# Heads of a gated delta rule in a fixed order on three engines, with right sides summed in PSUM and an inverse completed in two halves

## The chip, the cores and the metric

The kernel runs on one core of a Trainium2 chip. The metric is the device time of the core in microseconds, the median of three runs. A profile is of one execution.

## The reference

One residual block of a hybrid network on 1024 tokens of width 1024. After a normalisation, one projection feeds two branches, a gated linear attention (GLA, 4 heads) and a gated delta rule (GDN, 8 heads of 128). They are merged through sigmoid gates, projected, and followed by a squared-ReLU MLP. The change is in the GDN heads:

```python
d_qkv = jax.nn.silu(causal_short_conv(d_qkv, gdn_conv_w))   # 4 taps
d_q, d_k = l2_norm(d_q), l2_norm(d_k)
...
a_mat = jnp.where(strict, jnp.einsum('bhnid,bhnjd->bhnij', kb, k) * decay_mat, 0.0)
rhs = jnp.concatenate([v * beta[..., None], kb * jnp.exp(gc)[..., None]], axis=-1)
sol = lax.linalg.triangular_solve(a_mat + eye, rhs, left_side=True, lower=True)
u, w = sol[..., :dv], sol[..., dv:]
att = jnp.einsum('bhnid,bhnjd->bhnij', q, k) * decay_mat

def step(state, inp):                                        # over chunks
    v_new = uu - w @ state
    o = q_dec @ state + att @ v_new
    state = dec * state + k_state.T @ v_new
    return state, o

o_d = rms_norm(o_d, gdn_onorm_w) * jax.nn.silu(d_g)
```

## The kernel before

Activations lie transposed in SBUF, channels on partitions and 1024 tokens along the free axis. Dense products are computed with operands split into a high and a low part (`hH`, `hL` for the activations, `wH`, `wL` for weights): for each of 8 slices k of the contracted axis, three pairs of 128x512 matmuls, `hH,wH`, `hL,wH` and `hH,wL`. `dense_b` (L406) does one block of 128 output channels in that way. After each k it calls `tick()`: the clock of the program moves on by one, and functions that were entered in an agenda with `at(ticks, function)` for that time are issued. So small work is placed between dense work by hand: a tick is the time of three dense pairs, and each block has eight of them.

A GDN head (`gdn_head`, L741) has three dense blocks, for q (`psq`), v (`psv`) and the gate (`psg`), 24 ticks in all. Around them, in the agenda:

- the chunk's inverse `U` of 128x128 is completed from two solved 64x64 blocks: u1 transposes on VectorE, u2 and u3 are 8 products of 64x64 each on TensorE, with `yn` on VectorE between them;
- q and v pass the convolution (a scaled copy on ScalarE, then three taps on VectorE, all into `cv`) and silu; `att` makes the attention of 8 chunks of 128 tokens, `token_sums` the sums of squares of q by way of `sqt` and `sqr`;
- `kb` (scaled keys, VectorE) and `U` give `WT` (two groups on TensorE, copied by ScalarE); v is transposed and scaled into `bv`;
- a chain over the 8 chunks, one every three ticks: c1(t) sums `U`·`bv` and `WT`·`st` in PSUM and ScalarE takes it out as `vn`; c2(t), a tick later, makes the new state `st` (VectorE) and the output `po`, which ScalarE squares and copies to `ob`;
- at the end the norm (14 small steps and a product with `ob` on VectorE), 16 transposes of 32x256 to `obT`, and a product with the gate `si` (`fin`).

The chain of head h starts when its three dense blocks are through, and so lies beside the dense blocks of head h+1. Its last c2 is in the last tick of that head, and `fin` lies in the head after. `aacc` is a sum on VectorE for the modulation, that goes on beside all this, `wL` the low part of a weight tile, for the next dense block. GLA's last transposes (from `go`) fall into head 0.

An object `InOrder` stands in front of each engine and records each operation (so all have L38 in the profile). With its flag `strict` set, each operation is told to stay behind the one that the program wrote before it on that engine. In the heads the flag is off, and a scheduler, working from its own estimates, orders each engine's instructions.

Of the kernel before, what the change touches and what calls it, by code (L numbers as in the profile page):

```python
# [8 lines left out]
F32 = mybir.dt.float32  # L9
# [41 lines left out]
def block_kernel(ctx: ExitStack, tc: tile.TileContext, x, c, ada_w, ada_b, pre_mix_w, post_mix_w,  # L51
# [332 lines left out]
    plan += [(w_in, c0 + h * 128, 128, 8, V) for h in range(8) for c0 in (C_DQ, C_DV, C_DG)]  # L384
    plan += [(w, j * 256, 256, 8, None) for w in (w_bgla, w_bgdn) for j in range(4)]

    def splits():
        for w, c0, n, kt, E in plan:
            raw = load_raw(w, c0, n)
            if kt == 4:  # L390
# [95 lines left out]
    be_d = dr.tile([8, 1024], F32, name="be_d")  # L486
    dec_d = dr.tile([64], F32, name="dec_d")
# [5 lines left out]
    beC = cp.tile([128, 64], F32, name="beC")  # L493
    decB = cp.tile([128, 64], F32, name="decB")
# [189 lines left out]
    def key_norms():  # L684
        V.tensor_scalar(ssK, ssK, EPS, None, ALU.add)
        r = rsqrt(ssK, 64)
        V.tensor_mul(rbC, r, betaC)
        V.tensor_mul(beC, beC, r)
        V.scalar_tensor_tensor(beC, beC, -1.0, rbC, ALU.mult, ALU.mult)
        V.scalar_tensor_tensor(nbrC, rbC, -1.0, r, ALU.mult, ALU.mult)  # L690
        ps = pat()
        T.transpose(ps[0:64, 0:128], nbrC, ident)
        nb = t4((128, 128), p="nbr")
        V.tensor_copy(nb[0:64], ps[0:64, 0:128])
        ST.dma_start(be_d.rearrange("h (t q) -> (h t) q", q=128), nb[0:64])
# [45 lines left out]
    def gdn_head(h):  # L741

        U = Ub[h % 2]
# [4 lines left out]
        DMA.dma_start(a21, a21_d[h])  # L748
        kT, Dt = t4(p="kT"), t4(p="Dt", tag="hd")
        DMA.dma_start(kT, kT_d[h])  # L750
        DMA.dma_start(Dt, Dt_d[h])
        z = {}

        def u1():
            t11 = z["t11"] = t4((64, 8, 64), p="t11")
            lo, hi = slice(0, 32), slice(32, 64)
            for a_ in (lo, hi):
                for b_ in (lo, hi):
                    V.transpose(t11[b_, :, a_], U[a_, :, b_])

        def u2():
            py = pat()
            for t in range(NT):
                T.matmul(py[64:128, t * 64:(t + 1) * 64], a21[:, t, :], z["t11"][:, t, :], start=True, stop=True)
            z["yn"] = t4((128, 8, 64), p="yn")
            V.tensor_tensor(z["yn"][64:128], py[64:128, :].rearrange("p (t q) -> p t q", t=8),
                            colb(nbrC[64:128, h * 8:h * 8 + 8], 8, 64), ALU.mult)

        def u3():
            pu = pat()  # L770
            for t in range(NT):
                T.matmul(pu[0:64, t * 64:(t + 1) * 64], z["yn"][64:128, t, :], U[64:128, t, 64:128], start=True, stop=True)
            A.copy(U[0:64, :, 64:128], pu[0:64, :].rearrange("p (t q) -> p t q", t=8))

        at(5, u1)
        at(9, u2)
        at(11, u3)
        psq = dense_b(h_rhs)

        q = silu_half(conv(psq, h))  # L780
        vq = small(8, "vq")
        qj = t4(p="qj")
        attT = t4(p="attT")

        def att(hf):
            pt = pat()
# [3 lines left out]
            V.tensor_mul(attT[:, hf * 512:(hf + 1) * 512], pt, Dt[:, hf * 512:(hf + 1) * 512])  # L790

        at(6, lambda: att(0))
        at(7, lambda: att(1))
        at(8, lambda: A.activation(qj, q, AF.Square))
        token_sums(qj, vq, QT, EPS)
# [3 lines left out]
        kb = t4(p="kb")  # L799
        if h == 7:  # L800
            oa_s.plan(range(9, 17), 8)
        at(5, lambda: V.tensor_tensor(r3(kb), r3(ktok), colb(beC[:, h * 8:h * 8 + 8], 8), ALU.mult))
        psv = dense_b(h_rhs)

        A.activation(eg, eg, AF.Exp)
        vv = silu_half(conv(psv, 16 + h))
        bv = t4(p="bv")
        V.tensor_tensor(eg, q, eg, ALU.mult)
        qd = eg

        WT = t4(p="WT")

        def wt_(hf):
            pt = pat()
            for i in range(4):
                t = hf * 4 + i
                T.matmul(pt[:, i * 128:(i + 1) * 128], kb[:, t * 128:(t + 1) * 128], U[:, t, :], start=True, stop=True)
            A.copy(WT[:, hf * 512:(hf + 1) * 512], pt)

        at(2, lambda: wt_(0))  # L820
        at(3, lambda: wt_(1))

        def vt_(hf):
            pt = pat()
            for i in range(4):
                t = hf * 4 + i
                T.transpose(pt[:, i * 128:(i + 1) * 128], vv[:, t * 128:(t + 1) * 128], ident)
            V.tensor_tensor(r3(bv)[:, hf * 4:hf * 4 + 4, :], r3(pt, 4),
                            colb(rbC[:, h * 8 + hf * 4:h * 8 + hf * 4 + 4], 4), ALU.mult)

        at(6, lambda: vt_(0))
        at(7, lambda: vt_(1))
        psg = dense_b(h_rhs)

        sg = silu_twice(psg)
        ob = t4(p="ob")
        so = small(8, "so")
        c = {"st": None}

        def c1(t):  # L840

            sl = slice(t * 128, (t + 1) * 128)
            pv = pat()
            T.matmul(pv[:, :128], U[:, t, :], bv[:, sl], start=True, stop=(t == 0))
            if t:
                T.matmul(pv[:, :128], WT[:, sl], c["st"], start=False, stop=True)

            v2 = c["vn"] = sm.tile([128, 256], F32, tag="gst", name=nm("vn"), bufs=3)
            if t < NT - 1:
                A.activation(v2[:, 0:128], pv[:, :128], AF.Copy, scale=ksC[:, h * 8 + t:h * 8 + t + 1])  # L850
            A.copy(v2[:, 128:256], pv[:, :128])

        def c2(t):
            sl = slice(t * 128, (t + 1) * 128)
            i, hf, st, vs, vn = t % 4, t // 4, c["st"], c["vn"][:, 0:128], c["vn"][:, 128:256]
            if t < NT - 1:
                pS = pat()
                T.matmul(pS[:, :128], ktok[:, sl], vs, start=True, stop=True)
                sn = c["st"] = sm.tile([128, 128], F32, tag="st", name=nm("st"), bufs=3)
                if t:  # L860
                    V.scalar_tensor_tensor(sn, st, decB[:, h * 8 + t:h * 8 + t + 1], pS[:, :128], ALU.mult, ALU.add)
                else:
                    A.copy(sn, pS[:, :128])
            if i == 0:
                c["po"] = pat()
            po = c["po"]
            T.matmul(po[:, i * 128:(i + 1) * 128], attT[:, sl], vn, start=True, stop=(t == 0))
            if t:
                T.matmul(po[:, i * 128:(i + 1) * 128], qd[:, sl], st, start=False, stop=True)
            if i == 3:  # L870
                for i in range(4):
                    t_ = hf * 4 + i
                    A.activation(ob[:, t_ * 128:(t_ + 1) * 128], po[:, i * 128:(i + 1) * 128], AF.Square,
                                 accum_out=so[:, t_:t_ + 1])
                A.copy(ob[:, hf * 512:(hf + 1) * 512], po)
            if t == NT - 1:

                V.tensor_scalar(so, so, 1.0 / 128, None, ALU.mult)
                V.scalar_tensor_tensor(so, vq, 128.0 * EPS, so, ALU.mult, ALU.add)
                rf = rsqrt(so, 8)  # L880
                V.tensor_tensor(r3(ob), r3(ob), colb(rf, 8), ALU.mult)

        obT = t4(p="obT")

        def fin(q):
            blocks(r3(obT), r3(ob), (32 * q,))
            if q == 3:
                V.scalar_tensor_tensor(sg, obT, don, sg, ALU.mult, ALU.mult)
# [978 lines left out]
```

## Time and profile before

| | us |
|---|---|
| median of 3 runs | 1967.45 |
| lowest, highest | 1963.69, 1969.73 |
| the profiled execution | 1963.2 |
| its span | 1961.5 |
| TensorE's busy time | 1921.7 |
| mean granted clock of TensorE | 0.994 |

The heads of the GDN run from about 665 to 1062 us of the span. In rows of the timeline the first number is the start, the second the time from the first instruction's start to the last one's end, then the engine, the operation, what it writes and reads, and a count; matmuls overlap, so their pace is read from starts.

### The profile page before, as it was taken

The page shows a single profiled execution, that of the slowest core. Times are in us where ns is not written, and L with a number is a line of the kernel's source. Part 1 is how long each engine was busy: PE and PEld are TensorE (multiplying, and loading weights), DVE is VectorE, ACT ScalarE, POOL GpSimd, SP SyncE. Part 2 cuts the span into 40 slices and gives each one's busy share as a digit, 9 for nine tenths or more (in the row PEclk, how much of TensorE's full clock was granted, in tenths as well). Part 3 has the DMA queues.
Part 4 walks back from the last instruction along what each step waited for, and adds up shares of the span by engine and source line. Part 5 has one row for each costly group of instructions (what it writes and reads, how often), then busy time and mean ns, then how long its engine had stood idle before and what let it go on. Part 6 is the DMA issues. An engine that isn't in the chain of part 4 may idle for free.

```text
span 1961.5 us, 26008 instructions
## 1 busy us (share of the span) xinstructions
PE 1921.7 (98%) x9894; PEld 1622.6 (83%) x9894; DVE 1447.3 (74%) x2653; ACT 801.9 (41%) x1427; POOL 172.1 (9%) x120
## 2 busy tenths in 40 slices
PE   5999999999999999999999999999999999999998
PEld 4788888889899888888888888888888888888886
DVE  7867599658769697888787434666668886787887
ACT  5554323342342333333336231247644446343333
POOL 3300100310110100000001110000012220000001
PEclk8999999999999999999999999999999999999999
DMA  9365622423222433333358785244666767452525
GB/s 295 111 211 178 202 101 84 143 65 108 60 70 76 143 111 105 116 117 114 96 162 208 184 192 124 102 131 159 205 216 214 245 228 258 158 204 66 202 97 97
DMA packets 214444, 292.24 MB, mean 149 GB/s; under 512 B 33695, under 2 KB 153966, under 8 KB 214318
## 3 DMA queue, kind: packets, MB, share of 16 engines
q1 hardware_dynamic: 174910, 243.50, 38.1%
q10 hardware_dynamic: 21760, 35.01, 5.0%
q0 software_dynamic: 17648, 12.06, 4.7%
q8 instruction: 78, 1.28, 0.3%
q14 instruction: 48, 0.39, 0.1%
HBM read 215.42 MB, written 75.11 MB: 148 GB/s over the span
## 4 chain that ended last, share of the span: by engine, by line
PE 46%; DVE 3%; DMA 1%; ACT 0%; issue 0%; DVEq 0%; ACTq 0%
PE pa L38 23%; PE pm L38 23%; DVE obT L38 1%; DVE cv L38 0%; DMA sl<-sg_d 0%; DMA os<-oa_d 0%; DVE oL L38 0%; DVE rt L38 0%; DVE si L38 0%; DVE sqt L38 0%; DVE ya L38 0%; DVE rs L38 0%; DVE sqr L38 0%; DVE yg L38 0%; DVE st L38 0%
## 5 line engine op out<-in xcount | busy, mean ns | idle before, releaser
L38 PE MATMUL pm<-hH,wH 128*128 128x512 f32 x1008 | 327.6, 405 | 0.4 <-DVE cv L38 0.4
L38 PE MATMUL pm<-hL,wH 128*128 128x512 f32 x1008 | 314.5, 393 | 0.0
L38 PE MATMUL pm<-hH,wL 128*128 128x512 f32 x1008 | 313.5, 391 | 0.1
L38 PEld LDWEIGHTS pm<-hH,wL 128*128 128x128 f32 x1008 | 189.4, 188 | 41.8 <-DVE wL L38 0.5
L38 PEld LDWEIGHTS pm<-hL,wH 128*128 128x128 f32 x1008 | 189.6, 188 | 40.9
L38 PE MATMUL pa<-w,yH 128*128 128x512 f32 x688 | 212.1, 390 | 0.0
L38 ACT CAST wH<-raw 128x1024 fp32r<-128x1024 f32 x95 | 99.1, 1051 | 270.7 <-PE pm L38 189.1
L38 PEld LDWEIGHTS pm<-hH,wH 128*128 128x128 f32 x1008 | 176.7, 190 | 26.4 <-issue 1.1
L38 DVE TENSOR_TENSOR w<-raw,w 128x512 fp32r<-128x512 f32 (+1 forms) x142 | 123.4, 872 | 49.3 <-ACT w L38 48.5
L38 PEld LDWEIGHTS pa<-w,yH 128*128 128x128 f32 x688 | 129.1, 188 | 27.2 <-DVE ya L38 0.4
L38 ACT CAST w<-raw 128x512 fp32r<-128x512 f32 (+1 forms) x143 | 98.2, 708 | 88.9 <-DVE raw L38 79.8
L38 PE MATMUL pa<-w,yL 128*128 128x512 f32 x344 | 133.9, 389 | 0.0
L38 PE MATMUL pa<-oB,w 128*128 128x512 f32 x480 | 111.4, 390 | 0.0
L38 DVE SCALAR_TENSOR_TENSOR cv<-pm,ccol,cv 128x1023 f32<-128x1023 f32 (+2 forms) x72 | 92.1, 1280 | 24.2 <-ACT cv L38 23.1
L38 DVE TENSOR_TENSOR wL<-raw,wH 128x1024 fp32r<-128x1024 f32 x72 | 88.5, 1236 | 26.9 <-ACT wH L38 26.6
L38 PEld LDWEIGHTS pa<-oB,w 128*128 128x128 f32 x480 | 89.8, 188 | 18.5 <-DVE w L38 0.2
L38 PE MATMUL pa<-oT,w 128*128 128x512 f32 x384 | 90.8, 389 | 0.0
L38 PE MATMUL pm<-oT,w 128*128 128x512 f32 x384 | 90.8, 389 | 0.0
L38 DVE TENSOR_TENSOR ya<-pa,ya 128x512 f32<-128x512 f32 x82 | 55.9, 689 | 43.3 <-PE pa L38 43.3
L38 PEld LDWEIGHTS pa<-oT,w 128*128 128x128 f32 x384 | 72.1, 188 | 14.9
L38 PEld LDWEIGHTS pm<-oT,w 128*128 128x128 f32 x384 | 72.1, 188 | 14.9
L38 PE MATMUL pm<-oH,wH 128*128 128x512 f32 x256 | 80.7, 396 | 0.0
(329 smaller groups left out, 3808.7 us busy)
## 6 DMA issues: line engine op xcount, KB each, us to landing
yL<-y_d SPq DMA_DIRECT2D x53, 512.0 KB
raw<-in_mlp_w_dram SPq DMA_DIRECT2D x23, 1024.0 KB
raw<-in_w_in_dram SPq DMA_DIRECT2D x19, 1024.0 KB
raw<-in_w_in_dram SPq DMA_DIRECT2D x34, 512.0 KB
araw<-in_ada_w_dram SPq DMA_DIRECT2D x32, 512.0 KB
raw<-in_mlp_w_dram SPq DMA_DIRECT2D x18, 512.0 KB
araw<-in_ada_w_dram SPq DMA_DIRECT2D x32, 256.0 KB
sg_d<-sig ACTq DMA_DIRECT2D x16, 512.0 KB
```

The costliest lines, as they stand in the source:

```text
L38: r = fn(*args, **kw)
```

## The change

**Order.** During the eight heads `strict` is on for TensorE, VectorE and ScalarE: these three carry out the program's order. Inside a head, ticks are now counted from its begin (`on`). The convolution's taps, tanh and silu have a tick each, the norm is at tick 48, its product at 49 and the transposes at 50 and 51 (before, in effect at 52, 53, 60 and 62). High and low parts of the heads' weights are made at given ticks (`conv_w_later`).

**Right sides.** `kb`, `bv` and `WT` are gone. `ke` holds the transposed keys with a negative factor for each token. c0(t) transposes a chunk of v into PSUM and adds `ke`·`st`; ScalarE takes the sum out with the factor beta as `rs`; c1(t), a tick later, is `U`·`rs`; c2(t) stays in the tick that it had.

**Inverse.** u2 and u3 alternate between the upper and the lower 64 rows and columns of the array, chunk by chunk, with a second copy of a block of `U` (`u22`) loaded for it. They come at ticks 7 and 9, before at 9 and 11.

The first place is on VectorE, where head h's finish (`ob`, `obT`) meets the chain of head h+1 (`st`). `sqt`, `sqr` and `vq` are the sums of squares of head h+1, `t` and `uw` the inverse's transposes of head h+2, `am` small steps of the modulation. Before:

```order
L38 TENSOR_TENSOR ob_7476<-ob_7476,rs_7869 128x1024
L38 TENSOR_REDUCE sqr_7938<-sqt_7937 128x16
L38 STREAM_TRANSPOSE obT_7478<-ob_7476 32x8x32 x8
L38 TENSOR_TENSOR am_123<-pa_7981,vcol 128x8
L38 SCALAR_TENSOR_TENSOR st_7994<-st_7943,decB,pa_7992 128x128
L38 SCALAR_TENSOR_TENSOR am_123<-am_123,vcol 128x8
L38 STREAM_TRANSPOSE t_7998<-U_5855 32x8x32 x4
L38 STREAM_TRANSPOSE obT_7478<-ob_7476 32x8x32 x8
L38 TENSOR_TENSOR wL_8210<-raw_8207,wH_8209 128x1024
L38 TENSOR_SCALAR vq_7611<-pa_8027 32x8 x4
L38 SCALAR_TENSOR_TENSOR st_8035<-st_7994,decB,pa_8033 128x128
L38 SCALAR_TENSOR_TENSOR si_7472<-obT_7478,vcol,si_7472 128x1024
```

and now:

```order
L38 SCALAR_TENSOR_TENSOR rs_7001<-rt_7002,rs_7001 128x8
L38 SCALAR_TENSOR_TENSOR si_7019<-si_7019,pm_6903 128x512 x2
L38 TENSOR_TENSOR ob_6815<-ob_6815,rs_7001 128x1024
L38 STREAM_TRANSPOSE obT_7055<-ob_6815 32x8x32 x16
L38 SCALAR_TENSOR_TENSOR si_6599<-obT_7055,vcol,si_6599 128x1024
L38 STREAM_TRANSPOSE sqt_7095<-qj_6884 128x512
L38 TENSOR_REDUCE sqr_7096<-sqt_7095 128x16
L38 SCALAR_TENSOR_TENSOR st_7110<-st_7065,decB,pa_7084 128x128
L38 STREAM_TRANSPOSE uw_7027<-U_5860 32x8x32 x4
```

The new state of c2(1) stood between two halves of the sixteen transposes, and the product with the gate stood behind the next state; now all of the finish is ahead of that state.

The second place is on TensorE at the same boundary, in the first c2 and c0 of head h+1 that use a state made by VectorE: `pm` rows are dense pairs, three to a tick.

```order
L38 MATMUL pa_7504<-vn_7520,kt_7175 128x128
L38 MATMUL pa_7487<-vn_7520,attT_7280 128x128
L38 MATMUL pa_7487<-st_7485,eg_7176 128x128
L38 MATMUL pm_7455<-hH_634,wH_7336 128x512 x2
L38 MATMUL pm_7455<-hL_635,wH_7336 128x512 x2
L38 MATMUL pm_7455<-hH_634,wL_7396 128x512 x2
L38 MATMUL pa_7547<-ident,cv_7318 128x128
L38 MATMUL pa_7547<-st_7530,ke_7179 128x128
L38 MATMUL pm_7455<-hH_678,wH_7336 128x512 x2
```

c2(1) is followed by one tick of dense work, and then c0(2) reads the state that VectorE makes from c2(1). In the program before, two ticks lay between:

```order
L38 MATMUL pa_7555<-vn_7542,kt_7188 128x128
L38 MATMUL pa_7519<-vn_7542,attT_7187 128x128
L38 MATMUL pa_7519<-st_7517,eg_7189 128x128
L38 MATMUL pm_7493<-hH_632,wH_7345 128x512 x2
L38 MATMUL pm_7493<-hL_633,wH_7345 128x512 x2
L38 MATMUL pm_7493<-hH_632,wL_7346 128x512 x2
L38 MATMUL pm_7493<-hH_676,wH_7345 128x512 x2
L38 MATMUL pm_7493<-hL_677,wH_7345 128x512 x2
L38 MATMUL pm_7493<-hH_676,wL_7346 128x512 x2
L38 MATMUL pa_7578<-bv_7340,U_5855 128x128
L38 MATMUL pa_7578<-st_7557,WT_7342 128x128
```

Each group of the chain moved from two groups and a free tick to three groups, one a tick. From the head's last c2 to that c0(2) the program has seven ticks of dense pairs, the groups c0(0), c1(0), c2(0), c0(1), c1(1) and c2(1), and the transpose of c0(2).

The third place is VectorE in head 0, from the first tap of q to the attention. Before:

```order
L38 SCALAR_TENSOR_TENSOR cv_5945<-pm_5871,ccol,cv_5945 128x1023
L38 SCALAR_TENSOR_TENSOR cv_5945<-pm_5871,ccol,cv_5945 128x1022
L38 SCALAR_TENSOR_TENSOR cv_5945<-pm_5871,ccol,cv_5945 128x1021
L38 TENSOR_TENSOR yn_5983<-pa_5974,nbrC 64x512
L38 STREAM_TRANSPOSE obT_5997<-go_5596 32x4x32 x3
L38 SCALAR_TENSOR_TENSOR cv_5945<-si_5950,cv_5945 128x1024
L38 STREAM_TRANSPOSE obT_5997<-go_5596 32x4x32 x13
L38 TENSOR_TENSOR kb_5960<-kt_5956,beC 128x1024
```

and now:

```order
L38 SCALAR_TENSOR_TENSOR cv_5961<-pm_5874,ccol,cv_5961 128x1023
L38 SCALAR_TENSOR_TENSOR cv_5961<-pm_5874,ccol,cv_5961 128x1022
L38 STREAM_TRANSPOSE obT_6008<-go_5601 32x4x32 x8
L38 SCALAR_TENSOR_TENSOR cv_5961<-pm_5874,ccol,cv_5961 128x1021
L38 TENSOR_TENSOR wL_6026<-raw_5970,wH_6000 128x1024
L38 STREAM_TRANSPOSE obT_6008<-go_5601 32x4x32 x8
L38 SCALAR_TENSOR_TENSOR si_5761<-obT_6008,vcol,si_5761 128x512
L38 SCALAR_TENSOR_TENSOR aacc_4592<-araw_5925,sc,aacc_4592 128x1024
L38 SCALAR_TENSOR_TENSOR cv_5961<-si_6024,cv_5961 128x1024
L38 TENSOR_TENSOR attT_6051<-pa_6052,Dt_5869 128x512
```

Silu of q (the `cv` from `si`), which stood behind three of the sixteen transposes of GLA, is now behind all of them, the weight's low part and `aacc`.

The diff, cut to its core:

```diff
-    plan += [(w_in, c0 + h * 128, 128, 8, V) for h in range(8) for c0 in (C_DQ, C_DV, C_DG)]
+    plan += [(w_in, c0 + h * 128, 128, 8, E) for h in range(8) for c0, E in ((C_DQ, (1, 6)), (C_DV, (1, 7)), (C_DG, (2, 4)))]
...
+    def conv_w_later(raw_ap, shape, dh, dl):
+        w = [None, None]
...
+        at(dh, high)
+        at(dl, low)
+        return w
...
+        begin = clock[0]
+        def on(t, fn):
+            at(begin + t - clock[0], fn)
...
+        halves = (slice(64, 128), slice(0, 64))
         def u2():
             py = pat()
             for t in range(NT):
-                T.matmul(py[64:128, t * 64:(t + 1) * 64], a21[:, t, :], z["t11"][:, t, :], start=True, stop=True)
...
+                T.matmul(py[halves[t % 2], t // 2 * 64:t // 2 * 64 + 64], a21[:, t, :], t11[:, t, :], start=True, stop=True)
+            V.tensor_tensor(yn, r3(py[:, 0:256], 4), colb(nbrX[:, h * 4:h * 4 + 4], 4, 64), ALU.mult)
...
-        at(5, u1)
-        at(9, u2)
-        at(11, u3)
+        on(5, u1)
+        on(7, u2)
+        on(9, u3)
...
+            for s_ in (1, 2, 3):
+                on(t + s_, lambda s_=s_: tap(s_))
+            on(t + 4, tanh)
+            on(t + 5, lambda: V.scalar_tensor_tensor(y, u["t"], 1.0, y, ALU.add, ALU.mult))
...
+        ke = t4(p="ke")
+        DMA.dma_start(ke, ner_d[h].partition_broadcast(128))
...
+        on(16, lambda: V.tensor_tensor(ke, kT, ke, ALU.mult))
+        on(28, lambda: token_part(0))
+        on(30, lambda: token_part(1))
+        on(32, token_total)
...
-        at(2, lambda: wt_(0))
-        at(3, lambda: wt_(1))
...
+        def c0(t):
+            sl = slice(t * 128, (t + 1) * 128)
+            pv = c["pv"] = pat()
+            T.matmul(pv[:, 0:128], vv[:, sl], ident, start=True, stop=(t == 0), is_transpose=True)
+            if t:
+                T.matmul(pv[:, 0:128], ke[:, sl], c["st"], start=False, stop=True)
+            rs = c["rs"] = sm.tile([128, 128], F32, tag="rs", name=nm("rs"), bufs=2)
+            A.activation(rs, pv[:, 0:128], AF.Copy, scale=rbC[:, h * 8 + t:h * 8 + t + 1])
         def c1(t):
-            T.matmul(pv[:, :128], U[:, t, :], bv[:, sl], start=True, stop=(t == 0))
-            if t:
-                T.matmul(pv[:, :128], WT[:, sl], c["st"], start=False, stop=True)
...
+            T.matmul(pv, U[:, t, :], c["rs"], start=True, stop=True)
...
         for t in range(NT):
-            at(3 * t + 1, lambda t=t: c1(t))
-            at(3 * t + 2, lambda t=t: c2(t))
-        for q in range(4):
-            at((28, 29, 36, 38)[q], lambda q=q: fin(q))
+            on(24 + 3 * t, lambda t=t: c0(t))
+            on(25 + 3 * t, lambda t=t: c1(t))
+            on(26 + 3 * t, lambda t=t: c2(t))
+        on(48, norm)
+        on(49, scale)
+        for i in range(4):
+            on((50, 50, 51, 51)[i], lambda i=i: fin(i))
...
+    for e in (T, V, A):
+        e.last, e.strict = e.recent, True
     for h in range(8):
         gdn_head(h)
+    for e in (T, V, A):
+        e.strict = False
```

More of the change, by code (lines that the diff above doesn't have):

```diff
@@ L748, in gdn_head @@
         DMA.dma_start(a21, a21_d[h])
+        uw = t4((128, 16, 64), p="uw")
+        t11, yn, u22 = uw[0:64, 0:8, :], uw[:, 8:12, :], uw[0:64, 12:16, :]
+        DMA.dma_start(u22, ud[1].rearrange("j (t e) i -> e j t i", e=2)[1])
         kT, Dt = t4(p="kT"), t4(p="Dt", tag="hd")
@@ L789, in att, with squares, token_part, token_total @@
                 T.matmul(pt[:, i * 128:(i + 1) * 128], kT[:, sl], q[:, sl], start=True, stop=True)
[L790 to L795, printed above, removed]
+            V.tensor_mul(z["att"][:, hf * 512:(hf + 1) * 512], pt, Dt[:, hf * 512:(hf + 1) * 512])
+        def squares():
+            z["qj"] = t4(p="qj")
+            A.activation(z["qj"], q, AF.Square)
+        def token_part(hf):
+            if not hf:
+                z["t"], z["r"] = t4(p="sqt"), small(32, "sqr", 2)
+            h_ = slice(hf * 512, (hf + 1) * 512)
+            V.transpose(z["t"][:, h_], z["qj"][:, h_])
+            V.reduce_sum(z["r"][:, hf * 16:(hf + 1) * 16], r3(z["t"][:, h_], 16), axis=mybir.AxisListType.X)
+        def token_total():
+            ps = pat()
+            T.matmul(ps[:, 0:32], quad.rearrange("p a b -> p (a b)"), z["r"], start=True, stop=True)
+            for i in range(4):
+                V.tensor_scalar(vq[32 * i:32 * i + 32], ps[32 * i:32 * i + 32, 0:32].rearrange("p (t c) -> p c t", c=4)[:, i],
+                                EPS, None, ALU.add)
         ktok, eg = t4(p="kt", tag="hd"), t4(p="eg")
@@ L809, in gdn_head @@
[L809 to L818, printed above, removed]
-        at(2, lambda: wt_(0))
-        at(3, lambda: wt_(1))
[L823 to L829, printed above, removed]
```

123 lines of the change are left out of this document (74 added, 49 removed).

## The prediction

> **What bounds the kernel now.** I read the page first, for the engine that has no idle time.
>
> ```profile
> PE 1921.7 (98%) x9894; PEld 1622.6 (83%) x9894; DVE 1447.3 (74%) x2653; ACT 801.9 (41%) x1427; POOL 172.1 (9%) x120
> PE   5999999999999999999999999999999999999998
> PEclk8999999999999999999999999999999999999999
> ```
>
> TensorE works 98% of the span, at nine tenths or more of its clock in all slices but the first. So the change pays in two coins only: TensorE time that it takes away or adds, and TensorE idle time. A busy share says nothing about a single wait, so next come the waits of TensorE in the stage that is changed (the heads, 664 to 1100 us), and two instants that give the length of a head: the group that writes the inverse's product from `t` and `a`, in head 1 and in head 7.
>
> ```profile
> PE pa L38 <- DVE yn L38: 4.9, 5, 1.3
> PE pa L38 <- DVE st L38: 0.7, 2, 0.5
> PE pa L38 <- ACT vn L38: 0.4, 1, 0.4
> PE pa L38 <- DVE bv L38: 0.4, 1, 0.4
> 722.65 1.14 PE L38 MATMUL pa<-t,a 64*64 64x64 f32 x16
> 1021.68 1.14 PE L38 MATMUL pa<-t,a 64*64 64x64 f32 x16
> 722.65:771.50 48.85, 48.77 (x293) 41.89 (x293) 36.54 (x65) 17.85 (x46) 0.00 (x0) 1.00 0.36 105
> ```
>
> Six heads take 1021.68 - 722.65 = 299.03 us, 49.8 each, and in all eight TensorE waits 4.9 + 0.7 + 0.4 + 0.4 = 6.4 us. The last row is one head (busy us of TensorE, its loads, VectorE, ScalarE, GpSimd, then clock): VectorE, the engine waited for, has 12 us free in a head. It is late at moments, not on the whole. Whether it is late after the change is therefore a question of order inside a head.
>
> **Taken from TensorE.** The `WT` groups go, two a head.
>
> ```profile
> 943.05 1.05 PE L38 MATMUL pa<-U,kb 128*128 128x128 f32 x8
> 943.86 0.71 PE L38 MATMUL pm<-hH,wH 128*128 128x512 f32 x2
> 944.41 0.63 PE L38 MATMUL pm<-hL,wH 128*128 128x512 f32 x2
> ```
>
> Eight records take 943.86 - 943.05 = 0.81, and the dense pair behind them 944.41 - 943.86 = 0.55, where a pair in the rows of a whole tick below takes a third of 1.38, 0.46: 0.09 more. So a group costs 0.90, a record 0.1125. The rest keeps its records: a head had 16 in `WT`, 8 transposes of `vv`, and 30 in c1, 54 in all; it will have 22 in c0 (8 transposes, 7 times 2 for `ke` by `st`) and 16 in c1, 38 in all. c2 and the attention stay. 16 records x 8 heads x 0.1125 = **-14.4**.
>
> The old waits of 6.4 go too: `bv` no longer exists, `yn` has two ticks before its reader and half the columns, and the wait for `st` is worked out anew below. **-6.4**. If `yn` were as late as before, 4.9 of this would stay.
>
> u2 and u3 of the inverse now go to alternating 64-row tiles.
>
> ```profile
> 677.54 1.14 PE L38 MATMUL pa<-t,a 64*64 64x64 f32 x16
> 678.61 0.73 PE L38 MATMUL pm<-hH,wH 128*128 128x512 f32 x2
> 539.27 0.33 PE L38 MATMUL pa<-zm,b 128*64 128x64 f32 x4
> 539.38 0.28 PE L38 MATMUL pa<-zm,ks 128*64 128x64 f32 x2
> 539.50 0.34 PE L38 MATMUL pa<-zm,b 128*64 128x64 f32 x4
> ```
>
> On one tile 16 records take 1.07, or 0.067 each. No row shows tiles that differ in rows and columns; the nearest alternates 64-column tiles, 6 records in 539.50 - 539.27 = 0.23, or 0.039 each. By that a group saves 16 x 0.028 = 0.45, and 16 groups **-7.2**. Bounds: two tiles wholly beside each other, 0.53 a group, -8.6; or a record as dear as one of 128x128, 0.1125, +11.7. I take the nearest row.
>
> **Hidden.** The row of one head shows ScalarE at 17.85 of 48.85 us: 64 more scalings to `rs` (about 0.28 each by the row below, 2.2 a head) find room, and the two copies to `U` replace one. The extra loads (`ke`, `u22`) go out on SP's queue eight and nine ticks, 11 us, ahead of use; the share of the DMA engines in that row is 0.36. Uncovered, a late `ke` would hold all of c0. The split weights now come up to two ticks before use, not eight: a late `wL` would cost up to its own 1.2. The store of `od` only moves forward, behind its producer on ScalarE's queue. The mixing of `kb` (1.2) becomes that of `ke`; two `bv` of 0.69 leave VectorE.
>
> **Added: the order on VectorE.** These are the rows at the end of a head, of TensorE, ScalarE and then VectorE.
>
> ```profile
> 1004.21 0.60 PE L38 MATMUL pa<-ident,cv 128*128 128x128 f32 x4
> 1006.04 0.62 PE L38 MATMUL pm<-hH,wH 128*128 128x512 f32 x2
> 1007.42 0.38 PE L38 MATMUL pa<-bv,U 128*128 128x128 f32 x2
> 1004.41 0.28 ACT L38 ACTIVATE ob<-pa 128x128 f32<-128x128 f32 x1 [2.01 <-PE pa L38]
> 1005.59 0.17 DVE L38 TENSOR_SCALAR so<-so 128x8 f32<-128x8 f32 x1
> 1007.61 0.17 DVE L38 TENSOR_TENSOR rt<-rs 128x8 f32<-128x8 f32 x1
> 1008.37 0.68 DVE L38 SCALAR_TENSOR_TENSOR si<-si,pm 128x512 f32<-128x512 f32 x1
> 1008.97 0.16 DVE L38 SCALAR_TENSOR_TENSOR rs<-rt,rs 128x8 f32<-128x8 f32 x1
> 1009.04 0.70 DVE L38 STREAM_TRANSPOSE sqt<-qj 128x512 f32<-128x512 f32 x1
> 1009.67 1.18 DVE L38 TENSOR_TENSOR ob<-ob,rs 128x1024 f32<-128x1024 f32 x1
> 1010.77 0.68 DVE L38 TENSOR_REDUCE sqr<-sqt 128x16 f32<-128x512 f32 x1
> 1016.13 0.35 DVE L38 SCALAR_TENSOR_TENSOR st<-st,decB,pa 128x128 f32<-128x128 f32 x1
> 1018.19 3.59 DVE L38 STREAM_TRANSPOSE obT<-ob 32x256 f32<-32x256 f32 x8
> 1021.82 1.29 DVE L38 SCALAR_TENSOR_TENSOR si<-obT,vcol,si 128x1024 f32<-128x1024 f32 x1
> 1023.02 0.68 DVE L38 TENSOR_SCALAR vq<-pa 32x8 f32<-32x8 f32 x4
> ```
>
> A tick (three dense pairs) is 1007.42 - 1006.04 = 1.38. The head's last c2 is over at 1004.21, where the transposes behind it start; the norm starts 1.38 later, when ScalarE's squares are in. Before, the scheduler put `st` of the next head's c2(1) between the two halves of the sixteen transposes (1016.13), and TensorE's waits for `st` were the 0.7 us above. In the changed program all of the old head's finish stands ahead of this `st`, as the first order excerpt shows. By starts, on VectorE: 14 small steps of the norm at (1007.61 - 1005.59)/11 = 0.18, 2.6; two `si` of 0.60, 1.2; `ob` 1.1; sixteen transposes at (1021.82 - 1018.19)/8 = 0.454, 7.25; the product with `si` 1.2; `sqt` 0.63 and `sqr` 0.60; `st` 0.35. Sum 14.9, so `st` is there 1.38 + 14.9 = 16.3 after the last c2.
>
> TensorE wants it sooner than before, since c0 comes a tick ahead of the old c1. Between the last c2 and the product of `ke` and `st` in c0(2) stand, by the second excerpt, 7 ticks (9.66) and 19 small records (2.14): 11.8. It is first in TensorE's queue, and all dense pairs behind it wait. **Stall 4.5, in the boundaries into heads 2 to 7 (6 of them): +27.0.** Boundaries with an `aacc` (row below, 1.3 each) in the pile are two: **+2.6**. Bounds: if the pile only lasted as in the quoted head (`st` done 12.3 after the last c2), 0.5 a boundary, 3; if VectorE also has a step of 1.3 running each time, 35.
>
> **Head 0** has GLA's transposes in its line; these are VectorE's, and the attention that reads the result.
>
> ```profile
> 668.37 5.04 DVE L38 STREAM_TRANSPOSE obT<-go 32x128 f32<-32x128 f32 x16
> 678.05 3.91 DVE L38 SCALAR_TENSOR_TENSOR cv<-pm,ccol,cv 128x1023 f32<-128x1023 f32 x3
> 683.68 1.23 DVE L38 SCALAR_TENSOR_TENSOR cv<-si,cv 128x1024 f32<-128x1024 f32 x1
> 690.88 1.28 DVE L38 SCALAR_TENSOR_TENSOR aacc<-araw,sc,aacc 128x1024 f32<-128x1024 f32 x1
> 686.85 1.05 PE L38 MATMUL pa<-cv,kT 128*128 128x128 f32 x8
> ```
>
> The scheduler let the three taps, then silu at 683.68, pass thirteen transposes. By the third excerpt they will not: from 678.05, taps 3.9, sixteen transposes 5.0, `wL` 1.2, `si` 0.7, `aacc` 1.25, silu 1.15 end at 691.3. TensorE is at the attention at 686.85, less the 0.45 saved in u2. **+4.9**, with 0 as the other end if the old order's margins held.
>
> **The clock.** Idle TensorE has a second price. One gap of 2.6 us shows it; the second row is the window of time behind it (busy us of the engines, then the granted clock).
>
> ```profile
> 82.39 0.66 PE L38 MATMUL pa<-ident,cv 128*128 128x128 f32 x4 [2.60 <-DVE cv L38]
> 83.48:86.90 3.42, 3.42 (x12) 2.72 (x11) 1.90 (x5) 3.17 (x15) 1.43 (x1) 0.50 0.29 119
> ```
>
> After it 3.42 us ran at clock 0.50: 1.71 of work lost. The gaps of up to 1.3 in the waits above left the clock at 9 tenths or more. A gap of 4.5 to 4.9 is nearer to the first; as a part of the slow window can fall into the gap itself I take 1.5 each, seven gaps, **+10.5** (bounds 0 and 2.4 each, 16.8).
>
> The Trainium skill ("TensorE: Matmul & The Clock Gate", Part 1, the table of clock states) has the clock fall only after at least one idle window of about 3.4 us. Taken as a wholly idle window, a gap of 4.5 holds one in a third of the phases, and the clock would cost 7 x 1.71 / 3 = 4 instead of 10.5, by an estimate from that page: a time of 1978, on the way to the rival without clock loss. The trace doesn't agree: its gap of 2.60 us was enough.
>
> **Sum.** -14.4 - 6.4 - 7.2 + 27.0 + 2.6 + 4.9 + 10.5 = **+17.0**. The profiled execution has a span of 1961.5 and a time of 1963.2, 4 below the median of 1967.45: 1980.2 on its own basis, **1984** on the median's.
>
> **Rivals.**
> - *The pile doesn't hold TensorE* (faster). The point is 11.8 - 1.38 = 10.4 us from norm to `st`. For it: before, 12.3 was nearly enough, and VectorE has 12 us free per head. Against: the rows add to 14.9, and nothing may pass. Then 1967.45 - 28.0, plus head 0's 4.9 and 1.5: **1946**. That TensorE isn't really kept in that place, because the writer's order is not the program's, is out: the excerpts are of the program.
> - *Stalls, but no clock loss*: 1984 - 10.5 = **1974**, just outside what counts as slower. For it: no gap in the heads' stage now is long enough to test it there.
> - *More of the same*: the tiles save nothing (+7.2), the clock costs 2.4 (+6.3): **1998**. A c0 comes one tick (1.38) behind the c2 that makes its `st`, so any VectorE step of 1.3 at the wrong moment adds to it, which the `aacc` row (1.3) makes likely.
> - *The change doesn't do what it says*: excluded for the order; the dropped groups are gone from it.
>
> **How the numbers follow.** Forecast 0.45, no clock loss 0.21, more 0.16, no stall 0.18. A measurement here tells a change of about 0.3%, 6 us, from none. Faster: the no-stall case, 0.18. The same: two thirds of the case without clock loss, 0.14. Slower: 0.68. The range leaves out most of the no-stall case and little above: from the 1974 case with half of its stalls (some 12 less) to just past the 1998 case, 1961 to 2002.
>
> **What would show it.** Right: in the changed profile TensorE's largest wait is for `st`, six times 4 to 6 us, once a head, with the sixteen `obT` directly ahead of it on VectorE; the wait for `cv` in head 0; a granted clock under 0.99 in the heads; heads of 51 to 53 us. Wrong: no wait for `st` over 1 us, or heads of 46 to 47. The tiles: u2 near 0.62 a group. It would all be wrong if a transpose or the norm ran much faster back to back than in these rows.

## The result and the profile after

The changed kernel takes 1998.4 us (median of 5 runs, 1993.46 to 1999.87) against 1967.45; the ratio is 1.015, with a 95% interval of 1.0131 to 1.0168. It is 31 us slower by the medians, 29.5 by the ratio, where 17 were forecast; the time is inside the range of 1961 to 2002. The page of the changed kernel's profile, the lines that answer to those of before:

```profile
span 1998.2 us, 25761 instructions
PE 1924.5 (96%) x9767; PEld 1616.0 (81%) x9767; DVE 1441.1 (72%) x2638; ACT 818.1 (41%) x1483; POOL 171.2 (9%) x120
PE   5999999999999898999989999999999999999998
PEclk8999999999999999889999999999999999999999
```

TensorE has fewer matmuls (9767, before 9894) and a little *more* busy time. That is the first sign of the clock: the same work takes longer in some stretches, and slices 17 and 18 show it. The waits of TensorE in the heads (655 to 1140 us; total, times, longest):

```profile
PE pa L38 <- DVE st L38: 29.1, 8, 5.7
PE pa L38 <- DVE cv L38: 5.4, 1, 5.4
PE pm L38 <- DVE cv L38: 2.7, 1, 2.7
PE pa L38 <- DVE uw L38: 0.3, 1, 0.3
```

The old waits for `yn`, `bv` and `vn` are gone, and 6.4 us of waiting has become 37.5. One boundary of heads in the timeline (start, us, instruction, idle time before it and who ended it), TensorE and then VectorE:

```profile
814.82 0.39 PE L38 MATMUL pa<-st,eg 128*128 128x128 f32 x2
826.77 0.27 PE L38 MATMUL pa<-ident,cv 128*128 128x128 f32 x1
831.53 0.80 PE L38 MATMUL pa<-st,ke 128*128 128x128 f32 x2 [4.49 <-DVE st L38]
816.42 0.17 DVE L38 TENSOR_SCALAR so<-so 128x8 f32<-128x8 f32 x1 [3.28 <-ACT ob L38]
821.38 7.18 DVE L38 STREAM_TRANSPOSE obT<-ob 32x256 f32<-32x256 f32 x16
828.60 1.28 DVE L38 SCALAR_TENSOR_TENSOR si<-obT,vcol,si 128x1024 f32<-128x1024 f32 x1
831.14 0.34 DVE L38 SCALAR_TENSOR_TENSOR st<-st,decB,pa 128x128 f32<-128x128 f32 x1
```

The next dense pair starts at 814.96, where the last c2 is over. TensorE has done c0(2)'s transpose at 827.04 (826.77 + 0.27), 12.1 us later, and then waits; VectorE starts the norm at 816.42 and has `st` ready at 831.48, 16.5 us after that c2. All sixteen transposes (821.38) and the product with `si` (828.60), the last step of the old head's finish, stand ahead of it. Where an `aacc` lies in the pile the wait is 5.69 and 5.58; in one boundary (941.53) it is 2.7, since sixteen small products of the modulation took 1.7 us of TensorE just before and filled that part of the wait.

What the wait does to the clock shows in windows of 3.41 us. The clock changes only at the edges of such windows: all changes of it in the heads are whole multiples of 3.413 us apart. The same boundary (length, then busy us of TensorE, its loads, VectorE, ScalarE, GpSimd; granted clock; DMA):

```profile
827.37:830.78 3.41, 0.00 (x0) 0.00 (x0) 3.31 (x6) 0.00 (x0) 0.00 (x0) 1.00 0.02 8
830.78:834.20 3.42, 2.67 (x7) 2.25 (x8) 3.31 (x8) 0.37 (x1) 0.00 (x0) 0.50 0.35 145
834.20:837.61 3.41, 3.41 (x23) 2.72 (x22) 2.82 (x4) 0.52 (x2) 0.00 (x0) 0.50 0.02 5
837.61:841.02 3.41, 3.41 (x13) 3.02 (x13) 1.78 (x7) 1.11 (x1) 0.00 (x0) 0.50 0.84 243
841.02:844.43 3.41, 3.41 (x30) 2.73 (x30) 2.05 (x2) 1.00 (x3) 0.00 (x0) 1.00 1.07 353
```

The third of these windows again, counting on TensorE only the products that read or write `uw` (u2, with 64 rows):

```profile
834.20:837.61 3.41, 1.12 (x16) 0.50 0.02 5
```

One gap is followed by three windows at half clock, 2.67 + 3.41 + 3.41 us of work of which half, 4.7 us, is lost. The wait of 4.49 costs 9.2. Added up in the same way over the heads, 21.9 us are lost to the clock; before, none were.

### The profile page after: what moved, and what is told of

Its sections match the earlier page's. It is cut to its first block, busy times and chain, and to the rows that moved or that the text cites. A ratio compares the mean times of both kernels' runs of the same rounds, so it can differ in the third digit from the quotient of the medians.

```text
span 1998.2 us, 25761 instructions
## 1 busy us (share of the span) xinstructions
PE 1924.5 (96%) x9767; PEld 1616.0 (81%) x9767; DVE 1441.1 (72%) x2638; ACT 818.1 (41%) x1483; POOL 171.2 (9%) x120
## 4 chain that ended last, share of the span: by engine, by line
PE 87%; DVE 8%; DMA 2%; ACT 1%; issue 1%; SPq 0%; DVEq 0%
PE pm L38 57%; PE pa L38 30%; DVE obT L38 3%; DVE si L38 1%; DMA araw<-in_ada_w_dram 1%; DVE cv L38 1%; DVE acc L38 1%; DMA gr<-gc_d 0%; DMA x<-in_x_dram 0%; DVE ob L38 0%; DVE lba L38 0%; DVE aacc L38 0%; DVE sqr L38 0%; DVE sqt L38 0%; SPq L227 0%
## 5 line engine op out<-in xcount | busy, mean ns | idle before, releaser
L38 PE MATMUL pm<-hH,wH 128*128 128x512 f32 x1008 | 335.2, 414 | 2.7 <-DVE cv L38 2.7
L38 ACT ACTIVATE rs<-pa,rbC 128x128 f32<-128x128 f32 x64 | 23.7, 370 | 147.7 <-PE pa L38 141.2
```

The lines of the kernel that those rows point to most:

```text
L38: r = fn(*args, **kw)
```

## The experiments

Each kernel ran beside the kernel before on the same chip, and its ratio is to that. "Waits" are TensorE's idle us between 655 and 1140 us of the profile; "clock" is the work lost there, the sum over short slices of TensorE's busy time by the part of the clock that was missing.

| kernel | median, us | ratio (95%) | waits | clock |
|---|---|---|---|---|
| before | 1967.45 | 1 | 6.4 | 0 |
| the change | 1998.4 | 1.015 (1.0131 to 1.0168) | 37.5 | 21.9 |
| 1 idle work in the waits | 1986.4 | 1.0101 (1.0074 to 1.0128) | 17.1 | 7.0 |
| 2 no flag | 1969.2 | 1.0014 (1.0002 to 1.0027) | 16.9 | 3.4 |
| 3 no flag, late finish | 1956.6 | 0.9947 (0.9927 to 0.9966) | 13.2 | 0 |
| 4 TensorE without flag | 1987.0 | 1.0102 (1.0081 to 1.0124) | 21.9 | 20.2 |
| 5 flag on TensorE alone | 2003.3 | 1.0182 (1.016 to 1.0204) | 47.3 | 13.4 |
| 6 spread | 1968.7 | 1.0013 (1.0000 to 1.0026) | 20.3 | 4.5 |
| 7 spread more | 1954.9 | 0.9938 (0.9917 to 0.9958) | 11.9 | 0 |
| 8 no pile | 1951.2 | 0.9917 (0.9898 to 0.9935) | 8.9 | 4.5 |
| 9 u2 a tick later | 1989.8 | one run | 36.3 | 15.3 |
| 10 seven, on one tile | 1960.6 | 0.9965 (0.9953 to 0.9978) | 10.6 | 0 |
| 11 seven, with GpSimd | 1957.2 | 0.9948 (0.9933 to 0.9963) | 12.9 | 0 |

Spans less waits and clock (and less the added work in 1) are 1934 to 1946 us in every kernel of the new form but the tenth, where part of the form is undone. So these two columns hold most of the differences, which are 52 us between the fastest and the slowest.

**1. Does the clock cost what the windows say?** The wait stays as long, and is filled with products that nobody reads.

```diff
             pv = c["pv"] = pat()
+            for _ in range(16 if t == 2 and 1 <= h <= 6 else 0):
+                T.matmul(pv[:, 384:512], ident, ident, start=True, stop=True)
```

> The changed kernel, with 16 idle products of the identity with itself (128x128, into unused columns of PSUM, read by nobody) put on TensorE ahead of c0(2) in heads 1 to 6, so that 3.6 us of each wait for st are filled with work. If the lost clock is a price of TensorE's idling, the half-clock stretches behind these waits (17.9 us of lost work in the profile of the changed kernel) go, the waits that are left are 0.9 to 2 us each, and the time falls by 16 to 18 us, to about 1981. If the low clock has another cause (heat, the position in the program), or costs nothing that ends up in the time, the time stays within 4 us of 1998.

The same boundary in its timeline:

```profile
824.37 3.73 PE L38 MATMUL pa<-ident 128*128 128x128 f32 x32
829.14 0.49 PE L38 MATMUL pa<-st,ke 128*128 128x128 f32 x2 [0.93 <-DVE st L38]
```

Work of 3.6 us and 0.93 of idling stand where 4.49 of idling stood, `st` is no sooner, and the clock stays at full behind it (the product itself takes 0.49, in the change 0.80). The lost clock falls from 21.9 to 7.0, the span from 1998.2 to 1983.6, the median by 12.0 (by the ratios 0.5%, 10 us), less than the 16 to 18 expected: head 0's gap (2.2 us of clock), one gap with an `aacc` (1.7) and the end of head 7 (3.0) still lowered the clock, and the added work outlasts the one short wait of 2.7. The price of the clock is shown to be one of idling; the wait itself, which this kernel keeps, is the other part.

**2. Is it the flag or the ticks?**

```diff
-    for e in (T, V, A):
-        e.last, e.strict = e.recent, True
...
-    for e in (T, V, A):
-        e.strict = False
```

> The changed kernel without the flag that keeps the three engines to the program's order; all ticks as in the change. If the order given by the ticks makes the stall, the sixteen transposes still stand ahead of st and the time is 1998 within 6 us, with waits for st of 4.5 us. If the flag makes it (the scheduler would otherwise let st pass), the waits for st shrink to under 1 us and the time is about 1950.

Neither expectation was right. The time is that of the kernel before, as if the ticks were harmless, but the waits don't vanish. TensorE and VectorE at the same boundary:

```profile
801.60 0.39 PE L38 MATMUL pa<-st,eg 128*128 128x128 f32 x2
813.61 0.27 PE L38 MATMUL pa<-ident,cv 128*128 128x128 f32 x1
815.21 0.68 PE L38 MATMUL pa<-uw,a 64*64 64x64 f32 x16
820.65 0.49 PE L38 MATMUL pa<-st,ke 128*128 128x128 f32 x2 [2.26 <-DVE st L38]
820.26 0.34 DVE L38 SCALAR_TENSOR_TENSOR st<-st,decB,pa 128x128 f32<-128x128 f32 x1
```

`st` is even later, 18.9 us after the last c2 (801.74 to 820.60), because the scheduler puts a weight's low part and the inverse's transposes into the norm. But between c0(2)'s transpose (813.61) and its product with `st` it lets the next u2 and eight dense pairs pass. TensorE idles 2.26 us, and four of the six gaps of this kind (0.9 to 2.3 us) leave the clock alone.

**3. Does a later finish take the wait away?**

```diff
-            on((50, 50, 51, 51)[i], lambda i=i: fin(i))
+            on((50, 51, 60, 70)[i], lambda i=i: fin(i))
```

> The kernel without the flag, and the four parts of the old head's finish at ticks 50, 51, 60 and 70 in place of 50, 50, 51, 51. If the pile of transposes ahead of st is the cause, the six waits for st (27.5 us) and the half clock behind them (18 us) go, and the time is 1950 to 1960; head 0's wait for cv stays. If VectorE simply has too much to do within three ticks, the waits come back at later states or at the attention, and the time stays above 1985.

1956.6, as expected: with eight of the sixteen transposes ahead of `st` instead of all, the wait is 1.3 to 1.5 us in five of the six boundaries, and the clock never falls in the heads. Head 0's wait for `cv`, which was expected to stay, is down to 1.4 without the flag. The kernel is 0.5% faster than the one before.

**4 and 5. Which engine's order?** In 4 the flag is on VectorE and ScalarE (`for e in (V, A)`), in 5 on TensorE alone (`for e in (T,)`).

> The changed kernel with the flag on VectorE and ScalarE alone. VectorE keeps the changed order, with all of the old head's finish ahead of st; on TensorE the scheduler puts two ticks of dense pairs ahead of the product of ke and st in c0(2). If TensorE's fixed order is what costs (a product that waits for st holds dense work that could run), the wait at c0(2) falls from 4.5 to about 1.7 us, the clock mostly holds, and the time is about 1965 (1960 to 1972). If VectorE's order is what costs, the time stays above 1985.

> The changed kernel with the flag on TensorE alone. TensorE reaches c0(2) 11.8 us after the old head's last c2, as in the change; VectorE, in the scheduler's order, also puts a weight's low part and the inverse's transposes into the finish, and in the kernel without the flag st was ready 18.9 us after the last c2. If TensorE's fixed order is what costs, the six waits for st are 6 to 7 us each and the time is 2005 to 2025, slower than the change. If VectorE's order is what costs, the time is that of the kernel without the flag, 1969.

Five came out as TensorE's fixed order said, six waits of 4.8 to 7.8 us. It is a little slower than the change (1.0182 against 1.015, with intervals that touch), since `st` is later:

```profile
826.09 0.27 PE L38 MATMUL pa<-ident,cv 128*128 128x128 f32 x1
832.89 0.80 PE L38 MATMUL pa<-st,ke 128*128 128x128 f32 x2 [6.53 <-DVE st L38]
```

The median of 2003.3 is just under the 2005 expected, because the clock cost less than in the change (13.4): here the gap itself covers most of the half windows. Four was expected at 1965 and took 1987. The wait at c0(2) is 2.0 as expected (1.7), but `wL`, `rs` and `uw` follow with waits of their own, 21.9 in all with `st`, and the clock still falls five times (seven in the change). One such window, with the end of a wait of 2.03 and two short ones in it (0.52 and 0.19), and the next:

```profile
774.81:778.22 3.41, 1.56 (x20) 1.14 (x20) 3.34 (x7) 1.10 (x4) 0.00 (x0) 1.00 0.74 298
778.22:781.64 3.42, 3.02 (x15) 2.51 (x11) 3.31 (x10) 0.80 (x1) 0.00 (x0) 0.50 0.49 154
```

So freeing TensorE alone gives back 11 us of 31 by the medians, freeing all three 29. The fixed orders of VectorE and ScalarE cost too once TensorE no longer runs in step with them. The longest of the new waits shows how: TensorE has passed `st` with dense pairs of two ticks and so comes to the next weight sooner, while VectorE makes its low part in its fixed place behind the pile and the state (`wL` at 834.25, TensorE waiting 1.94 for it until 835.52).

**6 and 7. Less ahead of the state.** Both without flags. Six has the finish at 50, 54, 60, 70 and the sums of squares at 33, 36, 42; seven has them at

```diff
+            on((50, 54, 60, 66)[i], lambda i=i: fin(i))
...
+        on(39, lambda: token_part(0))
+        on(42, lambda: token_part(1))
+        on(44, token_total)
```

> Without the flag, the finish at ticks 50, 54, 60 and 70 and the sums of squares at 33, 36 and 42 (28, 30 and 32 in the change), so that the scheduler puts st behind seven transposes and nothing else of the finish. st should be ready 10.5 us after the last c2, before TensorE asks for it. Theory: the waits for st that the kernel with finish at 50, 51, 60, 70 still had (10.9 us) go down to 1 to 3 us and the time to 1946 to 1950. Rival, VectorE is too full: the work that was moved delays a later state or the attention, and the time stays at 1956.

> As the one before, with the finish at ticks 50, 54, 60 and 66 and the sums of squares still later, at 39, 42 and 44. Theory: 1946 to 1950 as well, within 2 us of it, since neither is near its deadline. Rival: the sums come too late for the norm, which delays the finish and st by 1 to 2 us a head, 1956 to 1962.

In both, the wait at c0(2) falls to 0.2 to 0.4 us in most boundaries, but one of 1.0 appears at c0(3), in two heads of six and three of seven, where the other nine transposes and the product with the gate now stand ahead. Six has two more of 2.7 and 3.2 at later states, in two heads, and both lower the clock. Its time of 1968.7 is 13 above the rival's 1956 and 19 above the theory, and the reason isn't that VectorE is too full. VectorE stands idle just before the late states:

```profile
978.69 0.71 DVE L38 STREAM_TRANSPOSE sqt<-qj 128x512 f32<-128x512 f32 x1 [4.27 <-DMA od_d<-si]
982.26 0.34 DVE L38 SCALAR_TENSOR_TENSOR st<-st,decB,pa 128x128 f32<-128x128 f32 x1
```

By the profile `sqt`, whose tile comes out of the same pool as `si`, waits for the store of the finished `si`, which starts only when the finish is over. In three heads that takes 3.4 to 4.3 us, and the work that has gathered behind it delays `st`. Seven, with the finish four ticks earlier and `sqt` later, has no such wait. Seven, waits in the heads:

```profile
PE pa L38 <- DVE st L38: 6.6, 10, 1.0
PE pa L38 <- ACT vn L38: 2.5, 3, 1.6
PE pa L38 <- ACT rs L38: 1.4, 2, 0.8
PE pa L38 <- DVE cv L38: 1.4, 1, 1.4
```

At 1954.9 it is the fastest whole kernel here, 0.6% under the kernel before (interval 0.4 to 0.8%) and 2% under the change; three and eleven can't be told from it. It is above its 1946 to 1950, as 6.6 us of waits for `st` are left and not 1 to 3, and 5.3 of others.

**8. The fixed order without the pile.** All flags and ticks of the change stay.

```diff
-            if i == 0:
-                c["obT"] = t4(p="obT")
-            blocks(r3(c["obT"]), r3(c["ob"]), (32 * i,))
             if i == 3:
-                V.scalar_tensor_tensor(sg, c["obT"], don, sg, ALU.mult, ALU.mult)
```

> The changed kernel with all three flags and all ticks, but the sixteen transposes of ob and the product with the gate are left out (8.45 us of VectorE a head; the heads' results are then stored without them). If this pile ahead of st is what makes the fixed order dear, st is ready about 8 us after the last c2, TensorE asks for it at 11.8, the six waits (27.5 us) and the half clock behind them (17.9 us) go, and the time is 1950 to 1957; head 0's wait for cv (5.4 us and 2.5 of clock) stays. If the fixed order holds TensorE at any step that is late, waits appear at later states and the time stays above 1975.

1951.2, and in its profile the whole list of TensorE's waits in the heads:

```profile
PE pa L38 <- DVE cv L38: 5.4, 1, 5.4
PE pm L38 <- DVE cv L38: 2.7, 1, 2.7
PE pa L38 <- DVE st L38: 0.4, 1, 0.4
PE pa L38 <- DVE uw L38: 0.4, 1, 0.4
```

Two instants of its timeline, four heads apart:

```profile
816.89 0.68 PE L38 MATMUL pa<-uw,a 64*64 64x64 f32 x16
1002.93 0.68 PE L38 MATMUL pa<-uw,a 64*64 64x64 f32 x16
```

Not one wait is left in heads 2 to 7 but the last head's end, and a head takes (1002.93 - 816.89)/4 = 46.5 us, before 49.8. So in heads 2 to 7 the fixed order as such makes no wait; the pile ahead of `st` does, because nothing may pass it. The kernel leaves the pile's 8.45 us a head out and doesn't only move it, and no run keeps the flags and moves it: that a later place for the finish would do as well under the flags isn't shown.

**9. Why three half windows, and sometimes two?**

```diff
-        on(7, u2)
-        on(9, u3)
+        on(8, u2)
+        on(10, u3)
```

> The changed kernel with u2 and u3 one tick later (8 and 10). In the change's profile a window of 3.41 us at half clock that TensorE filled wholly was followed by full clock when products of 64 rows took up to 17% of it, and by another half window when they took 33%. If products of 64 rows count as little work for the clock, u2 now falls out of the second window behind a gap of 4.5 us, that window is followed by full clock, and such gaps have two half windows in place of three. If three windows come from the length of the gap, there are three again, with u2 anywhere.

The gaps are as long as in the change (4.49, 4.50, 4.48), and none is followed by three half windows. The windows of the second boundary:

```profile
821.23:824.64 3.41, 0.16 (x2) 0.00 (x0) 3.33 (x6) 0.00 (x0) 0.00 (x0) 1.00 0.00 0
824.64:828.05 3.41, 2.17 (x6) 1.88 (x7) 3.32 (x8) 0.37 (x1) 0.00 (x0) 0.50 0.82 287
828.05:831.47 3.42, 3.42 (x10) 2.74 (x10) 3.20 (x4) 0.53 (x2) 0.00 (x0) 0.50 0.47 147
831.47:834.88 3.41, 3.41 (x33) 2.83 (x33) 2.40 (x7) 1.12 (x1) 0.00 (x0) 1.00 0.78 232
```

The third of them is as full as in the change, holds no product of 64 rows, and full clock follows. The change has a boundary that lies almost the same way on the grid of windows (from 881.94): 7%, 62% and 100% busy, here 5%, 64% and 100%; a third of its full window was u2, and half clock followed. The lost clock is 15.3 in place of 21.9. It is one run, read window by window; its time, 1989.8, has no interval.

**10. The inverse's tiles.** Seven, with u2 and u3 as in the kernel before, on one tile.

> The kernel of the spread finish (50, 54, 60, 66; sums at 39, 42, 44; no flags), with the inverse's products back on one 64-row tile. Theory: a group takes 1.07 in place of 0.61 us, 16 groups, so 7 us more than that kernel: 1962, range 1960 to 1965. Rival: TensorE's time in u2 and u3 hides behind its waits for st and vn, and the time stays within 2 us of 1955.

```profile
770.62 1.14 PE L38 MATMUL pa<-uw,a 64*64 64x64 f32 x16
771.69 0.73 PE L38 MATMUL pm<-hH,wH 128*128 128x512 f32 x2
```

A group takes 1.07 again, and the median is 5.7 above seven's (by the ratios 0.27%, or 5.3 us, with intervals that overlap a little), with 1.3 us less of waits: close to the 7 expected.

**11. Some of VectorE's work on GpSimd.** Seven, with these two products moved.

```diff
-        on(15, lambda: V.tensor_tensor(qd, q, eg, ALU.mult))
-        on(16, lambda: V.tensor_tensor(ke, kT, ke, ALU.mult))
+        on(15, lambda: G.tensor_tensor(qd, q, eg, ALU.mult))
+        on(16, lambda: G.tensor_tensor(ke, kT, ke, ALU.mult))
```

> The kernel of the spread finish, with the products for ke and for the decayed q (eg) on GpSimd, which is idle in the heads; VectorE loses 2.4 us a head. Theory: the waits that are left for st (6.6 us) fall by half and the time to 1949 to 1953. Rival: GpSimd is late with them, or slows VectorE, and the time is 1956 or more.

The waits for `st` stay at 6.6, and the time (1957.2) can't be told from seven's. The theory's 1949 to 1953 didn't come, the rival's 1956 or more did, and the trace shows a part of the rival, that GpSimd slows VectorE. GpSimd takes 2.4 us for a product that took VectorE 1.2, and some of VectorE's operations beside it, which read two tensors from SBUF, get longer (GpSimd, then VectorE; silu takes 1.22 elsewhere):

```profile
781.61 2.39 POOL L38 TENSOR_TENSOR ke<-kT,ke 128x1024 f32<-128x1024 f32 x1 [43.70 <-DMA ke<-ner_d]
783.01 2.07 DVE L38 SCALAR_TENSOR_TENSOR cv<-si,cv 128x1024 f32<-128x1024 f32 x1 [2.57 <-ACT si L38]
```

So VectorE's busy time falls by 12.8 us (1438.6 to 1425.8) and not by the 19.5 of the sixteen products. Nor could the rest help `st`: VectorE has no backlog when the finish begins, as at 805.50 it has been idle for 3.84 us when it starts the norm (3.88 in seven). What makes `st` late at c0(3) is the work that stands between the norm and it, and none of that was moved.

## Why the prediction was right, and where its size was off

- **Taken from TensorE** (-14.4 and -7.2). Right. Two rows of the changed profile give the tile's group:

```profile
728.85 0.68 PE L38 MATMUL pa<-uw,a 64*64 64x64 f32 x16
729.47 0.73 PE L38 MATMUL pm<-hH,wH 128*128 128x512 f32 x2
```

  0.62 by these rows and 0.61 in the other groups at full clock, as the row of 64-column tiles had said (1.07 less 0.45), and the tenth kernel agrees in the time. For u2 that row was more than the nearest: by the kernel, both inputs of u2 lie on the lower-numbered 64 partitions, so its products alternate in the columns alone; only u3 alternates in rows and columns, as the text ahead of the prediction says of both. The dropped records show in the pace without stalls: the old head's 49.8 less its waits (6.4 in eight heads, 0.8) less 1.8 and 0.9 is 46.3, and the eighth kernel's heads take 46.5.
- **The old waits** (-6.4): gone, all of them.
- **The stall** (+27.0 and +2.6): 4.5 forecast, 4.49, 4.49 and 4.50 measured in the plain boundaries; 5.69 and 5.58 where an `aacc` lies in the pile. `st` came 16.5 us after the last c2 (16.3 forecast), and TensorE wanted it after 12.1 (11.8). The sixth boundary has 2.7, for the modulation's products. The six sum to 27.5, all waits for `st` to 29.1; that this is so near to 29.6 is in part luck, as two small waits that weren't forecast (1.2 and 0.4) make up for the short one. That it was the pile is shown by the eighth kernel; that free engines hide about half of the wait, by the second, and in the fourth, at this place, TensorE alone.
- **Head 0** (+4.9): 5.4, the wait for `cv`. VectorE has the two halves of GLA's transposes, `wL`, `si` and `aacc` ahead of that silu, as forecast.
- **The heads** (51 to 53 us): 53.9, as u2 of head 7 starts at 1052.08 and (1052.08 - 728.85)/6 = 53.9, about what the clock cost beyond the forecast.
- **The clock** (+10.5): 21.9. This is the term that was mis-sized, and the step that failed reads "I take 1.5 each": one half window to a gap, from the single gap of 2.60 us in the trace of before. The seven gaps that lowered the clock got one to three half windows each, 1.5 to 4.7 us of work. The bound of 2.4 a gap, 16.8 in all, was too low as well. That there were seven is luck: the boundary with the wait of 2.7 left the clock alone, and a gap at the end of head 7 that wasn't forecast lowered it.
- **Left out**: a wait of 2.7 at the end of head 7, where a tap late on VectorE holds the result of a dense block in PSUM, and 1.5 of its clock (in the 21.9); 0.3 for `uw`.

With the measured sizes the sum is -14.4 - 6.4 - 7.4 + 29.1 + 5.4 + 2.7 + 0.3 + 21.9 = +31.2, against +31.0 measured between the medians. So close an agreement is luck too: the waits and the clock are those of the profiled executions, whose spans differ by 36.7 (1998.2 against 1961.5), and some 5 us of that are not in the sum, 1.3 of them clock lost outside the heads (11.1 against 9.8). The two errors of the expectations that matter, two and four, are of one kind: they took one of two causes for the whole. The cost is made by two together, a late state on VectorE and a place on TensorE that nothing can pass.

Of the rivals, the one without clock loss fell with the windows and the first kernel, the one without a stall with the waits. *More of the same* named 1998, and the time is 1998.4, but only half by its mechanism: the clock did cost more, 21.9 and not its 16.8, while the tiles saved all that was forecast. The rule of the Trainium skill ("TensorE: Matmul & The Clock Gate", Part 1, the table of clock states), read as a wholly idle window, would by that estimate have made the clock's price 4, further off than the forecast: the windows of the change that lowered the clock were busy for 0 to 35% of their length, and two of the seven for none of it. What stays open is how much of the cost in kernel four comes from VectorE's fixed order and how much from ScalarE's; no run separates those two engines.

## What to carry to other kernels

Fixing an engine's order is harmless as long as everything that it waits for comes in time, and dear at the one place where it doesn't, since ready work stands behind; so count, for each consumer in a fixed order, what stands ahead of its producer on the other engine, in time and not in instructions. When the bounding engine idles, price the gap twice: once as itself, and once by the clock of the windows behind it, which at one gap here was as much again and over the heads 21.9 us for 37.5 of waits. A pile of work that has no deadline (here the finish of the head before) belongs behind the states that have one; here that gained 0.5% and 0.6% over the kernel before in two kernels without flags (3 and 7), while in a third (6) its latest place left nothing of the gain, since a later step had to wait for the store behind it.

## What the runs showed of the hardware

- TensorE's clock is granted by windows of 3.413 us on a fixed grid. In the heads, in the profiles of the change and the kernels 1 to 9, a window at full clock in which TensorE was busy for 43% or less was followed by half clock, one of 50% or more by full; between (45 to 48%) both occurred. No window has to be wholly idle for it.
- Coming back needs more. A window at half clock that was busy for up to 79% was followed by another one, one of 94% or more without products of 64 rows by full clock; of those at 84 to 90%, seven came back and one did not.
- Products on 64-row tiles seem to count for less. At half clock, fully busy windows with 24% or less of such products were followed by full clock, those with 33% or more by half. Moving u2 and u3 by one tick, and nothing else, left no gap of one run with a third half window, where three had one. That it is the size of the tile that counts, and not its pace, wasn't separated.
- A longer gap can cost less clock than a shorter one: in kernel five gaps of 6.5 us lost 1.4 to 1.5 of work each, in the change those of 4.5 lost 4.5 to 4.7, since in five one of the two half windows lay in the gap itself. With u2 a tick later gaps of 4.5 lost 1.7 to 2.9.
- Sixteen products of 64x64 take 1.07 us on one quarter of the array and 0.61 to 0.62 at full clock when they alternate, the same between two quarters beside each other on one set of 64 rows (u2) as between two opposite ones (u3).
- GpSimd slows some of VectorE's operations that read two tensors from SBUF: beside its products of 2.4 us, `cv` from `si` took 1.90 to 2.08 in three heads (1.22 elsewhere) and one `wL` 2.60 (1.22), while `st`, which reads one operand from PSUM, stayed at 0.35.
